# Moving the start of the settling loop and the gate steps in a streaming-encoder kernel

## The chip, the cores and the metric

The kernel is one program on one core of a Trainium2 chip. The metric is the device time of one execution in microseconds. The engines are PE (TensorE; PEld is its weight load), DVE (VectorE), ACT (ScalarE), POOL (GpSimd) and SP (SyncE). Each runs its own instructions in order and meets the others at semaphores. PE's clock has two levels, 1.2 and 2.4 GHz; the profile gives the granted clock as a share of the higher one.

## The reference

One layer of an encoder on 256 tokens of width 2048: a convolution group beside a state-space group, attention to 256 memory tokens, and a layer of single-neuron experts (PEER), with RMS norms between. The change lies in PEER. For each token and each of 8 heads, two lists of 128 keys give their 16 best; the 256 sums of the two give the 16 experts of the head. The gates are a softmax over the 16 scores, and

```python
u = jnp.take(u_tab, it, axis=0)
act = jax.nn.gelu(jnp.einsum("td,tkd->tk", xt, u))
v = jnp.take(v_tab, it, axis=0)
return jnp.einsum("tk,tkd->td", gt * act, v)
```

with tables of 16384 rows. So each token needs 128 scalar products with rows of `u_tab`, and the sum of 128 rows of `v_tab`.

## The kernel before

Tokens are handled as two halves of 128 (`tt` 0 and 1), tokens on partitions. The product with `u_tab` is split by columns.

- The first 768 columns are done densely, for all 16384 experts: `dense()` runs over 128 blocks of 128 experts. A block is loaded (`raw`, on SP's queue), transposed by PE into `ut` (6 transposes), copied from PSUM by ACT, and multiplied by the tokens (`sy`, 6 products). ACT then stores the results of two blocks at a time into two tables, `WA` for half 0 and `WB` for half 1.
- The other 1280 columns are gathered: `dot(j)` has POOL fetch one row for each token by an indirect DMA, and DVE multiplies and sums it (L895, here called a dot). There are 256 dots, 128 a half, with five gather buffers.

Before the dots of a group of heads can start, `Route` finds the chosen experts on DVE (`top16`, L789 to L797, and what follows). `gates()` ends the routing of a half: it writes `gate` from the scores, the features `fe` of the chosen indices, an exponential on ACT (L851), then on DVE a sum, a reciprocal, a product and `vidx` (L861 to L864), and on PE two transposes `ptc` (L867, L868) that ACT copies to `gT`. The features are stored to DRAM on SP (L1091) and loaded back in another layout (L906).

After the dense blocks, `settle()` picks for each token its 128 dense results out of the table. It goes by groups of 4 tokens, 32 groups a half. `extract` makes one-hot matrices E and H of the indices (matrix products `d` of 20 rows on PE, L962, then a ReLU on ACT, L964) and multiplies the table by E on PE (`y`, L970 for half 0, L973 for half 1). `pick` multiplies H by y on DVE (L980, here called a hit) and sums over partitions on PE (`more`, L982). While half 1 is settled, `left` and `build` also write half 0's coefficients back into the table (`dr`, `d`, R on DVE at L1005, `pw` on PE at L1008). Then `finish` for half 1 and its `build`s follow, and at last the dense product with `v_tab` (from L1150).

The order of the work around the change is set in two ways. DVE's order is the order in which the program calls it, written out by hand: the main loop asks for dots, and after each dot two `Pace` objects call the other generators at so many steps a dot (`ROUTE_RATE`, `DENSE_RATE`, `SETTLE_RATE`). At dot `SETTLE_AT` the settling takes the place of routing and dense work. The other engines' orders come from a planner that runs through the program with modelled times and puts each instruction where its operands are ready by the model. `LAG` is the number of groups by which `pick` runs behind `extract`. A pool's `bufs` says how many tiles of a tag may live at once: H, E, y and d have two each.

Of the kernel before, what the change touches and what calls it, by code (L numbers as in the profile page):

```python
# [9 lines left out]
F32 = mybir.dt.float32  # L10
# [4 lines left out]
AF = mybir.ActivationFunctionType  # L15
# [5 lines left out]
P = 128  # L21
# [40 lines left out]
TAIL_AT = 110  # L62
ROUTE_RATE = 4.0
DENSE_RATE = 0.8
SETTLE_RATE = 2.4
SETTLE_AT = 185
FEATS_AT = 150
LAG = 1
RAW_BUFS = 4
HI_BUFS = 3  # L70
LO_BUFS = 4
# [5 lines left out]
def trunk(ctx, tc, a, out, dbg=None):  # L77
    nc = tc.nc
    V, S, G, PE, SY = nc.vector, nc.scalar, nc.gpsimd, nc.tensor, nc.sync

    def bc(ap, shape):
        return ap.to_broadcast(shape)
# [55 lines left out]
    with ExitStack() as wctx:  # L138
        atx = wctx.enter_context(ExitStack())
        wp = wctx.enter_context(tc.tile_pool(name="wp", bufs=HI_BUFS, side="right"))  # L140
        at = atx.enter_context(tc.tile_pool(name="at", bufs=1))
# [68 lines left out]
        def run(g):  # L210
            for _ in g:
                pass
# [563 lines left out]
    class Route:  # L776
# [70 lines left out]
        def gates(self):  # L847
            self.gate = gate = rt.tile([P, PH, TOPK], F32, name="gate", bufs=2)
            gs = rt.tile([P, 2, PH], F32, name="gs")
            V.tensor_sub(gate, self.tm, bc(self.tm[:, :, 0:1], [P, PH, TOPK]))  # L850
            S.activation(gate, gate, AF.Exp)  # L851
            sq = rt.tile([P, 2, NSLOT], F32, name="sq")
            II = self.II.rearrange("p s h k -> p s (h k)")
            V.tensor_mul(sq, II, II)
            V.tensor_copy(fe[:, 0], sq)
            V.tensor_sub(fe[:, 1], sq, fe[:, 0])
            V.tensor_copy(fe[:, 2], II)
            stores.append((tick[0] + 12, self.tt))
            for _ in range(6):
                yield  # L860
            V.tensor_reduce(gs[:, 0], gate, axis=AX.X, op=ALU.add)  # L861
            V.reciprocal(gs[:, 1], gs[:, 0])
            V.tensor_mul(gate, gate, bc(gs[:, 1, :, None], [P, PH, TOPK]))
            V.tensor_scalar(vidx[self.tt], self.uidx.rearrange("p h k -> p (h k)"), float((DC - DU) // GU), None,  # L864
                            op0=ALU.add)
            pt = psu.tile([P, 2, P], F32, name="ptc", tag="pw", bufs=1)
            PE.transpose(pt[:, 0, :], gate.rearrange("p h k -> p (h k)"), ident)  # L867
            PE.transpose(pt[:, 1, :], self.II[:, 1].rearrange("p h k -> p (h k)"), ident)  # L868
            self.gT = lr_p.tile([P, 2, P], F32, name="gT", bufs=2)
            S.copy(self.gT, pt)  # L870
            yield
# [29 lines left out]
    fe_dram = [dram.tile([P, FEAT * 2 * NSLOT], BF16, name=f"fe_dram{tt}") for tt in range(NTT)]  # L901

    def load_feats(tt):
        src = fe_dram[tt].rearrange("(b j i) (f x) -> b (i f) j x", b=4, i=4, f=FEAT)
        for b in range(4):
            SY.dma_start(fe_at[tt][32 * b:32 * b + NROW].rearrange("f j s k -> f j (s k)"), src[b])  # L906
# [6 lines left out]
    fe = lr_p.tile([P, FEAT, 2, NSLOT], BF16, name="fe", bufs=1)  # L913
# [37 lines left out]
    def feats(route, g):  # L951
        p0 = 32 * (g // 8)
        return fe_at[route.tt][p0:p0 + NROW, g % 8], C[p0:p0 + NROW]

    def extract(route, g):
        psq, lr_q = settling_pools
        f, cs = feats(route, g)
        one = []
        for s, nm in ((1, "E"), (0, "H")):
            d = psq.tile([P, 4, P], F32, name="d")  # L960
            for i in range(4):
                PE.matmul(d[:, i, :], cs[:, i, :], f[:, s, :], start=i == 0, stop=i == 3, skip_group_check=True)  # L962
            one.append(lr_q.tile([P, 4, P], F32, name=nm))
            S.activation(one[-1], d, AF.Relu)  # L964
        E, H = one
        y = psq.tile([P, 4, P], F32, name="y")
        for i in range(4):
            t = 4 * g + i
            if route.tt == 0:
                PE.matmul(y[:, i, :], W[0][:, t, :], E[:, i, :], start=i == 0, stop=i == 3, skip_group_check=True)  # L970
            else:
                for h in range(2):
                    PE.matmul(y[64 * h:64 * h + 64, i, :], by_token[:, h, t, :], E[:, i, :], start=i == 0, stop=i == 3,  # L973
                              skip_group_check=True)
        return H, y

    def pick(route, g, H, y):
        if g == 0:
            route.more = psu.tile([P, NSLOT], F32, name="more", bufs=1)
        V.tensor_mul(H, H, y)  # L980
        for i in range(4):
            PE.matmul(route.more[i * NQ:(i + 1) * NQ, :], onecol[:, NQ - g:2 * NQ - g], H[:, i, :], start=g == 0,  # L982
                      stop=g == NQ - 1)

    def left(route, g):
        psq, lr_q = settling_pools
        f, cs = feats(route, g)
        dr = psq.tile([P, 4, P], F32, name="dr")
        PE.matmul(dr, f[:, 0, :], cs, start=True, stop=True)
        tag, bufs = ("L", 3) if route.tt == 0 or g % 2 else ("H", 2)  # L990
        L = lr_q.tile([P, 4, P], F32, name="L", tag=tag, bufs=bufs)
        if route.tt and g % 2:
            V.tensor_tensor(L, bc(iota[:, None, :P], [P, 4, P]), bc(route.gT[:, 1, 4 * g:4 * g + 4, None], [P, 4, P]),
                            op=ALU.is_equal)
        else:
            d = psq.tile([P, 4, P], F32, name="d")
            PE.matmul(d, f[:, 1, :], cs, start=True, stop=True)
            S.activation(L, d, AF.Relu)
        return dr, L

    def build(route, g, dr, L):
        psq, lr_q = settling_pools
        ts = slice(4 * g, 4 * g + 4)
        R = lr_q.tile([P, 4, P], F32, name="R", tag="E" if route.tt and g % 2 else "R", bufs=2)
        V.scalar_tensor_tensor(R, dr, 0.0, bc(route.cT[:, ts, None], [P, 4, P]), op0=ALU.max, op1=ALU.mult)  # L1005
        pw = psq.tile([P, 4, P], F32, name="pw", tag="y") if route.tt and g % 2 else psu.tile([P, 4, P], F32, name="pw")
        for i in range(4):
            PE.matmul(pw[:, i, :], L[:, i, :], R[:, i, :], start=i == 0, stop=i == 3, skip_group_check=True)  # L1008
        S.copy(W[route.tt][:, :, ts], pw.rearrange("p t b -> p b t"))

    routes = [Route(0), None]
# [27 lines left out]
    def settle():  # L1039
        groups = P // 4  # L1040
        for tt in range(NTT):
            held, lefts = {}, []
            for n in range(groups + LAG):
                if n < groups:
                    held[n] = extract(routes[tt], n)
                    yield
                if n >= LAG:
                    pick(routes[tt], n - LAG, *held[n - LAG])
                    yield
                if tt:  # L1050
                    if n:
                        build(routes[0], n - 1, *lefts.pop())
                    if n < groups:
                        lefts.append(left(routes[0], n))
                    yield
            if tt == 0:
                while tick[0] <= NSLOT:
                    yield
                yield from routes[0].finish()

    stores, tick = [], [0]
    routing = route_all()
    with tc.high_priority(offset=2000):
        while (0, 0) not in ready:
# [5 lines left out]
    for tt in range(NTT):  # L1070
        for g in range(len(GROUPS[tt])):
            while (tt, g) not in ready:
                next(routing)
            h0, n = routes[tt].heads(g)
            for j in range(h0 * TOPK, (h0 + n) * TOPK):
                if tick[0] == SETTLE_AT:
                    run(routing)
                    run(dense_gen)
                    psd_x.close()
                    lr_d_x.close()  # L1080
                    settling_pools += [
                        psx.enter_context(tc.tile_pool(name="psq", bufs=2, space=PSUM, reuse_waits="tile")),
                        lr_x.enter_context(tc.tile_pool(name="lr_q", bufs=2, side="right", reuse_waits="tile"))]
                    load_feats(1)
                    settling = settle()
                    paces = [Pace(settling, SETTLE_RATE)]
                routes[tt].dot(j)
                tick[0] += 1
                if stores and stores[0][0] == tick[0]:
                    tt_ = stores.pop(0)[1]  # L1090
                    SY.dma_start(fe_dram[tt_], fe.rearrange("p f s k -> p (f s k)"))  # L1091
                if tick[0] == FEATS_AT:
                    load_feats(0)
                for p in paces:
                    p()
# [115 lines left out]
```

## Time and profile before

| | |
|---|---|
| median of 3 runs | 2145.14 us (2144.22 to 2150.43) |
| profiled execution | 2155.07 us, span 2153.3 us |
| PE, PEld, DVE busy | 2030.7 (94%), 1722.3 (80%), 1709.3 (79%) us |
| ACT, POOL busy | 984.3 (46%), 763.0 (35%) us |
| mean granted clock of PE | 0.946 |

The profiled execution has 1.8 us around its span and lies 9.9 us above the median. PE is the busiest engine nearly everywhere; in the page's row of the granted clock, 40 slices of 54 us, the one slice well below full is at 1.31 to 1.47 ms, where the settling of half 0 runs. Busy shares are means over stages with different limits, so the stages are shown apart below. In the timeline a dot is a row of L895 followed by a short DVE_READ_ACCUMULATOR; matmuls in fp32 are counted as two instructions.

### The profile page before, as it was taken

To read this page: it belongs to the slowest core of one execution; us is meant where nothing else is said; L and a number is where in the kernel's file an instruction comes from. 1 tells how busy PE (TensorE), PEld (TensorE's weight loads), DVE (VectorE), ACT (ScalarE), POOL (GpSimd) and SP (SyncE) were. 2 spreads that over 40 slices of the span, in tenths; PEclk is the share of its full clock that TensorE was granted. 3 is DMA by queue.
4 is the path that set the end of the run, shared out by engine and by line. 5 is a ranking of instruction groups with operands and counts; after the bars stand their busy time and mean duration, and the time that the engine had idled before them with its cause. 6 is when DMAs were issued, how large, how long until landed. Compare 5 with 4: busy or idle time off the path is not lost.

```text
span 2153.3 us, 33240 instructions
## 1 busy us (share of the span) xinstructions
PE 2030.7 (94%) x12347; PEld 1722.3 (80%) x12347; DVE 1709.3 (79%) x2773; ACT 984.3 (46%) x1561; POOL 763.0 (35%) x576
## 2 busy tenths in 40 slices
PE   8998999997999999979999996999999999999996
PEld 7987786875899879868888885777667888888885
DVE  5889998995755568999966666556867899899998
ACT  5755666544544444323333332335654444444444
POOL 1000111000000004444555475222206777677775
PEclk9999999998999999989999996558999999999998
DMA  7656788776654658999899999456708999999996
GB/s 240 172 176 171 215 225 226 205 215 200 232 182 151 209 192 287 329 313 324 301 402 405 388 404 301 147 170 188 219 15 326 358 333 340 348 338 339 336 339 231
DMA packets 197875, 564.69 MB, mean 262 GB/s; under 512 B 31042, under 2 KB 37043, under 8 KB 197586
## 3 DMA queue, kind: packets, MB, share of 16 engines
q1 hardware_dynamic: 133842, 306.69, 42.5%
q0 software_dynamic: 63872, 255.89, 34.9%
q8 instruction: 97, 1.59, 0.3%
q14 instruction: 64, 0.52, 0.1%
HBM read 550.05 MB, written 12.45 MB: 261 GB/s over the span
## 4 chain that ended last, share of the span: by engine, by line
PE 61%; DVE 17%; issue 10%; POOL 5%; DMA 4%; ACT 2%; SPq 0%; POOLq 0%; DVEq 0%; ACTq 0%
PE acc L1159 8%; PE acc L1158 8%; PE acc L1157 8%; DVE u L895 5%; POOL u L893 5%; PE mm L195 4%; PE mm L194 4%; PE mm L196 4%; PE pw L1008 3%; PE mm L205 3%; PE mm L203 3%; PE mm L204 3%; PE y L970 3%; PE d L962 2%; PE y L973 2%
## 5 line engine op out<-in xcount | busy, mean ns | idle before, releaser
L895 DVE SCALAR_TENSOR_TENSOR u<-u,hnF 128x1280 f32<-128x1280 f32 x256 | 390.7, 1528 | 92.1 <-DMA u<-in_peer_u,uidx 89.8
L1122 POOL DMA_INDIRECT v<-in_peer_v,vidx x256 | 386.1, 1508 | 193.6 <-DVE accg L1124 84.4
L893 POOL DMA_INDIRECT u<-in_peer_u,uidx x256 | 300.8, 1175 | 397.4 <-DVE u L895 326.0
L942 PE MATMUL sy<-hnT,ut 128*128 128x256 f32 x1536 | 356.1, 384 | 22.1 <-ACT ut L938 21.0
L180 ACT CAST w_hi<-w_raw 128x1024 fp32r<-128x1024 f32 (+2 forms) x228 | 231.7, 1018 | 258.2 <-PE mm L196 124.2
L942 PEld LDWEIGHTS sy<-hnT,ut 128*128 128x128 f32 x1536 | 286.3, 192 | 62.5 <-ACT ut L938 25.0
L185 DVE TENSOR_TENSOR w_lo<-w_raw,w_hi 128x1024 fp32r<-128x1024 f32 (+2 forms) x204 | 239.7, 1177 | 106.9 <-ACT w_hi L180 106.5
L101 ACT CAST vh<-vr 128x1472 fp32r<-128x1472 f32 x128 | 183.1, 1431 | 251.9 <-PE acc L1158 207.1
L1158 PE MATMUL acc<-vh,wl 128*128 128x512 f32 (+1 forms) x768 | 295.4, 385 | 0.0
L1159 PE MATMUL acc<-vl,wh 128*128 128x512 f32 (+1 forms) x768 | 293.8, 385 | 0.5 <-DVE vl L102 0.5
L205 PE MATMUL mm<-aT_hi,w_lo 128*128 128x256 f32 x960 | 271.1, 289 | 16.2 <-DVE w_lo L185 8.3
L1157 PE MATMUL acc<-vh,wh 128*128 128x512 f32 (+1 forms) x768 | 275.7, 383 | 2.8 <-ACT vh L101 2.8
L203 PE MATMUL mm<-aT_hi,w_hi 128*128 128x256 f32 x960 | 274.2, 288 | 4.2 <-ACT w_hi L180 4.2
L204 PE MATMUL mm<-aT_lo,w_hi 128*128 128x256 f32 x960 | 271.9, 285 | 0.0
L102 DVE TENSOR_TENSOR vl<-vr,vh 128x1472 fp32r<-128x1472 f32 x128 | 216.6, 1693 | 41.6 <-ACT vh L101 39.4
L1124 DVE SCALAR_TENSOR_TENSOR accg<-v,coef,accg 128x576 f32<-128x576 f32 x256 | 208.5, 815 | 8.1 <-DMA accg<-h_dram 4.0
L205 PEld LDWEIGHTS mm<-aT_hi,w_lo 128*128 128x128 f32 x960 | 181.9, 192 | 24.3 <-DVE w_lo L185 11.3
L203 PEld LDWEIGHTS mm<-aT_hi,w_hi 128*128 128x128 f32 x960 | 184.6, 193 | 8.4 <-ACT w_hi L180 5.2
L204 PEld LDWEIGHTS mm<-aT_lo,w_hi 128*128 128x128 f32 x960 | 184.9, 193 | 2.4 <-issue 1.2
L1158 PEld LDWEIGHTS acc<-vh,wl 128*128 128x128 f32 x768 | 144.6, 188 | 30.3
L1157 PEld LDWEIGHTS acc<-vh,wh 128*128 128x128 f32 x768 | 144.6, 188 | 28.7 <-ACT vh L101 3.0
L183 POOL DMA_DIRECT2D w_lo<-in_w_kv_mem x24 | 29.3, 1221 | 384.5 <-ACT w_lo L182 277.0
(368 smaller groups left out, 3378.5 us busy)
## 6 DMA issues: line engine op xcount, KB each, us to landing
vr<-in_peer_v SPq DMA_DIRECT2D x128, 736.0 KB
raw<-in_peer_u SPq DMA_DIRECT2D x128, 384.0 KB
w_raw<-in_w_kv_mem SPq DMA_DIRECT2D x64, 512.0 KB
w_raw<-in_w_in SPq DMA_DIRECT2D x48, 512.0 KB
w_raw<-in_w_out SPq DMA_DIRECT2D x32, 512.0 KB
w_raw<-in_w_q_mem SPq DMA_DIRECT2D x32, 512.0 KB
w_raw<-in_w_o_mem SPq DMA_DIRECT2D x32, 512.0 KB
w_lo<-in_w_kv_mem POOLq DMA_DIRECT2D x24, 512.0 KB
```

Source lines behind the costliest of these rows:

```text
L180: S.copy(hi, raw)
L185: V.tensor_sub(lo, raw, hi.bitcast(F32))
L203: PE.matmul(o, wh, ah, start=first and cb % 2 == 0, stop=False, skip_group_check=True)
L204: PE.matmul(o, wh, al, start=False, stop=False, skip_group_check=True)
L205: PE.matmul(o, wl, ah, start=False, stop=last and end, skip_group_check=True)
L893: G.indirect_dma_start(out=u, out_offset=None, in_=a["peer_u"].rearrange("e (q c) -> (e q) c", c=GU), in_offset=bass.IndirectOffsetOnAxis( ...
L895: V.scalar_tensor_tensor(u, u, 1.0, hnF[:, self.tt, :], op0=ALU.mult, op1=ALU.mult, accum_out=self.act[:, j:j + 1])
L942: PE.matmul(ps[:, b % 2, :], ut[:, k, :], hnT[:, k, :], start=k == 0 and b % 2 == 0, stop=k == KD - 1 and b % 2 == 1, skip_group_check=True)
L1122: G.indirect_dma_start(out=v, out_offset=None, in_=table, in_offset=bass.IndirectOffsetOnAxis(ap=vidx[tt][:, j:j + 1], axis=0))
L1157: PE.matmul(o, wh[:, tt, :], vh[:, cs_], start=b == 0, stop=False)
L1158: PE.matmul(o, wl[:, tt, :], vh[:, cs_], start=False, stop=False)
L1159: PE.matmul(o, wh[:, tt, :], vl[:, cs_], start=False, stop=b == NB - 1)
```

## The change

The settling starts at dot 176 in place of 185, at 2.2 steps a dot in place of 2.4. For half 0 picks run two groups behind the extracts in place of one; for half 1 still one. For groups 2 and 3 of every four of half 0, H takes the buffers of tag R and y those of tag dr, which the settling of half 0 does not use otherwise, so that four H and four y can live at once. Of the gate steps, the exponential and the store of the features are asked for 16 dots after the scores are ready (the store was asked for 12 dots later, the exponential at once), the DVE steps 4 dots after that, and the transposes 16 dots later again.

```diff
-SETTLE_RATE = 2.4
-SETTLE_AT = 185
+SETTLE_RATE = 2.2
+SETTLE_AT = 176
-LAG = 1
+LAG = (2, 1)
+DELAY = 16
...
-            S.activation(gate, gate, AF.Exp)
...
-            stores.append((tick[0] + 12, self.tt))
-            for _ in range(6):
+            tasks.append((tick[0] + DELAY, self.softmax(gs)))
+            yield
+
+        def softmax(self, gs):
+            gate = self.gate
+            S.activation(gate, gate, AF.Exp)
+            SY.dma_start(fe_dram[self.tt], fe.rearrange("p f s k -> p (f s k)"))
+            for _ in range(4):
                 yield
             V.tensor_reduce(gs[:, 0], gate, axis=AX.X, op=ALU.add)
...
+            for _ in range(DELAY):
+                yield
             pt = psu.tile([P, 2, P], F32, name="ptc", tag="pw", bufs=1)
...
+        spread = route.tt == 0 and g % 4 > 1
...
-            one.append(lr_q.tile([P, 4, P], F32, name=nm))
+            one.append(lr_q.tile([P, 4, P], F32, name=nm, tag="R" if spread and nm == "H" else nm))
...
-        y = psq.tile([P, 4, P], F32, name="y")
+        y = psq.tile([P, 4, P], F32, name="y", tag="dr" if spread else "y")
...
-                if n >= LAG:
-                    pick(routes[tt], n - LAG, *held[n - LAG])
+                if n >= lag:
+                    pick(routes[tt], n - lag, *held[n - lag])
...
+                    for _, task in tasks:
+                        run(task)
...
-                if stores and stores[0][0] == tick[0]:
...
+                for at, task in tasks:
+                    if tick[0] >= at:
+                        next(task, None)
```

On DVE, after half 1's gate steps, the first hits (H) stood behind 113 further dots, the 187th dot of the program being the last before them:

```order
L863 TENSOR_TENSOR gate<-gate,gs 128x128
L864 TENSOR_SCALAR vidx_8372<-uidx 128x128
L895 SCALAR_TENSOR_TENSOR u,act<-u,hnF 128x1280 x113
L980 TENSOR_TENSOR H<-H,y 128x512
L895 SCALAR_TENSOR_TENSOR u,act<-u,hnF 128x1280
L980 TENSOR_TENSOR H<-H,y 128x512 x2
```

Now the same rows read so; half 1's gate steps come 17 dots later, and the first hit follows the 178th dot:

```order
L869 TENSOR_TENSOR gate<-gate,gs 128x128
L870 TENSOR_SCALAR vidx_8372<-uidx 128x128
L903 SCALAR_TENSOR_TENSOR u,act<-u,hnF 128x1280 x87
L989 TENSOR_TENSOR H<-H,y 128x512
L903 SCALAR_TENSOR_TENSOR u,act<-u,hnF 128x1280
L989 TENSOR_TENSOR H<-H,y 128x512
```

The first hit moved nine dots forward. Counted on, the 32nd hit follows dot 206 (before 212), the 33rd dot 209 (before 216), the 64th and last dot 251 (before 254).

On ACT, where the dense work of half 0's gate steps stands, the exponential came behind the copy of the 23rd block's `ut`, and the copy of `gT` behind that of the 26th:

```order
L938 COPY ut<-ut 128x768 x2
L851 ACT_TABLE_LOAD
L851 ACTIVATE gate<-gate 128x128
L945 COPY WA<-sy 128x128x2
L946 COPY WB<-sy 128x128x2
L938 COPY ut<-ut 128x768 x2
L945 COPY WA<-sy 128x128x2
L946 COPY WB<-sy 128x128x2
L938 COPY ut<-ut 128x768
L870 COPY gT<-ptc 128x256
```

Now these rows are:

```order
L946 COPY ut<-ut 128x768 x2
L863 ACT_TABLE_LOAD
L863 ACTIVATE gate<-gate 128x128
L953 COPY WA<-sy 128x128x2
L954 COPY WB<-sy 128x128x2
L946 COPY ut<-ut 128x768 x2
L953 COPY WA<-sy 128x128x2
L954 COPY WB<-sy 128x128x2
L946 COPY ut<-ut 128x768 x2
```

The exponential of half 0 has not moved: the planner still puts it behind the 23rd `ut`. The copy of `gT` has gone from behind the 26th to behind the 43rd. Half 1's exponential has come forward by one block, from behind the 59th `ut` to behind the 58th, and its `gT` has gone back from the 62nd to the 73rd.

On PE, the transposes of half 0's gates stood behind the 26th block's transposes:

```order
L942 MATMUL sy<-hnT,ut 128x256 x6
L936 MATMUL ut<-ident,raw 128x128 x6
L867 MATMUL ptc<-ident,gate 128x128
L868 MATMUL ptc<-ident,II 128x128
L942 MATMUL sy<-hnT,ut 128x256 x6
```

Now they stand behind the 43rd block's, in a stretch that reads alike:

```order
L950 MATMUL sy<-hnT,ut 128x256 x6
L944 MATMUL ut<-ident,raw 128x128 x6
L875 MATMUL ptc<-ident,gate 128x128
L876 MATMUL ptc<-ident,II 128x128
L950 MATMUL sy<-hnT,ut 128x256 x6
```

That is 17 blocks later, while the DVE steps that they wait for went from behind dot 35 to behind dot 53. Half 1's went from behind the 62nd block's transposes to behind the 72nd block's products, and their DVE steps from behind dot 74 to behind dot 91. In the settling, PE's order had the products y of two groups ahead of the first `more`; now it has those of four. On SP the store of half 0's features still stands behind the 27th `raw`, that of half 1 behind the 63rd (before the 64th).

## Rows read from the trace of the kernel before

**Rows 1.** Windows by stage: busy us of PE, PEld, DVE, ACT, POOL, clock, DMA, GB/s.
```profile
850.00:1303.00 453.00, 428.09 (x2310) 376.01 (x2310) 366.15 (x763) 144.94 (x261) 240.80 (x188) 0.98 0.96 355
1303.00:1325.00 22.00, 5.50 (x51) 3.90 (x50) 14.74 (x21) 3.92 (x8) 12.72 (x11) 0.68 0.98 313
1325.00:1432.00 107.00, 105.89 (x712) 80.61 (x712) 56.74 (x83) 32.19 (x58) 26.29 (x27) 0.50 0.57 177
...
1468.00:1570.00 102.00, 98.24 (x1133) 70.17 (x1129) 80.98 (x121) 61.88 (x110) 27.18 (x29) 1.00 0.64 194
```

**Rows 2.** Timeline as the dense work ends: start, us, engine, line, operation [idle before <-releaser].
```profile
1303.14 0.61 PE L962 MATMUL d<-hnF,C 20*128 20x128 bf16 x8
...
1303.64 1.49 DVE L895 SCALAR_TENSOR_TENSOR u<-u,hnF 128x1280 f32<-128x1280 f32 x1 [0.54 <-DMA u<-in_peer_u,uidx]
...
1304.45 1.16 PE L970 MATMUL y<-E,WA 128*128 128x128 f32 x8
...
1306.62 1.16 PE L970 MATMUL y<-E,WA 128*128 128x128 f32 x8 [0.46 <-ACT E L964]
...
1313.24 1.49 DVE L895 SCALAR_TENSOR_TENSOR u<-u,hnF 128x1280 f32<-128x1280 f32 x1 [2.79 <-DMA u<-in_peer_u,uidx]
...
1325.28 0.68 DVE L980 TENSOR_TENSOR H<-H,y 128x512 f32<-128x512 f32 x1
...
1326.11 0.65 PE L982 MATMUL more<-H,onecol 128*32 128x128 f32 x8 [15.76 <-DVE H L980]
```

**Rows 3.** Windows of 5 us: the clock's fall in settling and at its end.
```profile
1310.00:1315.00 5.00, 0.35 (x4) 0.17 (x3) 1.96 (x4) 0.00 (x0) 0.94 (x1) 0.60 1.05 293
...
1565.00:1570.00 5.00, 4.29 (x41) 2.42 (x40) 3.54 (x5) 3.04 (x6) 0.00 (x0) 1.00 0.00 0
1570.00:1575.00 5.00, 3.31 (x11) 2.35 (x12) 4.56 (x9) 0.54 (x2) 0.00 (x0) 0.54 0.50 153
```

**Rows 4.** Timeline of DVE: three hits of half 0, the last being its 32nd.
```profile
1396.66 0.69 DVE L980 TENSOR_TENSOR H<-H,y 128x512 f32<-128x512 f32 x1 [1.46 <-PE y L970]
...
1400.21 0.69 DVE L980 TENSOR_TENSOR H<-H,y 128x512 f32<-128x512 f32 x1 [1.46 <-issue]
...
1432.19 0.69 DVE L980 TENSOR_TENSOR H<-H,y 128x512 f32<-128x512 f32 x1 [2.87 <-PE y L970]
```

**Rows 5.** Timeline of DVE: the 33rd hit, the 64th, and the last two dots.
```profile
1443.26 0.68 DVE L980 TENSOR_TENSOR H<-H,y 128x512 f32<-128x512 f32 x1
...
1566.46 0.69 DVE L980 TENSOR_TENSOR H<-H,y 128x512 f32<-128x512 f32 x1 [2.62 <-PE y L973]
...
1567.67 1.48 DVE L895 SCALAR_TENSOR_TENSOR u<-u,hnF 128x1280 f32<-128x1280 f32 x1
...
1569.07 1.49 DVE L895 SCALAR_TENSOR_TENSOR u<-u,hnF 128x1280 f32<-128x1280 f32 x1
```

**Rows 6.** Timeline: the two exponentials on ACT, and PE behind each.
```profile
938.66 0.31 ACT L851 ACTIVATE gate<-gate 128x128 f32<-128x128 f32 x1 [14.60 <-DVE gate L850]
...
940.26 5.49 PE L942 MATMUL sy<-hnT,ut 128*128 128x256 f32 x12 [11.89 <-ACT ut L938]
...
1063.50 0.31 ACT L851 ACTIVATE gate<-gate 128x128 f32<-128x128 f32 x1 [8.76 <-DVE gate L850]
...
1065.10 4.54 PE L942 MATMUL sy<-hnT,ut 128*128 128x256 f32 x12 [4.76 <-ACT ut L938]
```

**Rows 7.** Timeline: dots 53 and 91, block 43's and 73's transposes, one gate step.
```profile
942.76 0.28 DVE L861 TENSOR_REDUCE gs<-gate 128x8 f32<-128x128 f32 x1
...
998.07 2.56 DVE L895 SCALAR_TENSOR_TENSOR u<-u,hnF 128x1280 f32<-128x1280 f32 x1
...
1001.07 0.82 PE L936 MATMUL ut<-ident,raw 128*128 128x128 f32 x6
...
1105.48 1.49 DVE L895 SCALAR_TENSOR_TENSOR u<-u,hnF 128x1280 f32<-128x1280 f32 x1
...
1105.97 0.82 PE L936 MATMUL ut<-ident,raw 128*128 128x128 f32 x6
```

More of the change, by code (lines that the diff above doesn't have):

```diff
@@ L1042, in settle @@
             held, lefts = {}, []
-            for n in range(groups + LAG):
+            lag = LAG[tt]
+            for n in range(groups + lag):
                 if n < groups:
@@ L1059, in settle @@
                 yield from routes[0].finish()
-    stores, tick = [], [0]
+    tasks, tick = [], [0]
     routing = route_all()
@@ L1088, in trunk @@
                 tick[0] += 1
-                if stores and stores[0][0] == tick[0]:
-                    tt_ = stores.pop(0)[1]
-                    SY.dma_start(fe_dram[tt_], fe.rearrange("p f s k -> p (f s k)"))
+                for at, task in tasks:
+                    if tick[0] >= at:
+                        next(task, None)
                 if tick[0] == FEATS_AT:
```

## The prediction

> **What bounds the kernel now.** I read the windows by stage first, then the timeline across their borders, then the waits. From 850 to 1303 us the dense work runs, and PE is busy 428.09 of 453 us at a clock of 0.98 [rows 1]. Then come 22 us in which PE does 5.50 us of work, and 107 us in which it is busy throughout, but at the lower of its two levels: 0.50, that is 1.2 GHz. The second half of the settling runs at 1.00, again with PE the busiest: 98.24 of 102 us, DVE 80.98. So each stage hangs on PE, and the weak spot is the join. The timeline shows why [rows 2]. PE starts the settling at 1303.14, has two groups' y done by 1308 and then finds its next instruction, a `more`, waiting 15.76 us for DVE: the hit stands behind dot 187 in DVE's order, and DVE gets there at 1325.28, one dot after another. The clock falls while PE waits (0.60 over 1310 to 1315, so about 1 us at full and 4 at half) [rows 3], and does not come back in half 0. At half clock a group takes 3.55 us, 1396.66 to 1400.21 [rows 4].
>
> **The gate steps.** The orders shown above decide this part more than the diff does. What stands in the way now is the exponential on ACT: it waits 14.60 us for DVE with the copies of `ut` behind it, and PE loses 11.89 us; half 1's waits 8.76 us and PE loses 4.76 [rows 6]. Half 0's exponential does not move, so its 11.89 us stay. Half 1's moves one block forward. PE then runs out of `ut` one block earlier, 453/128 = 3.5 us, less what DVE gains by having one dot fewer ahead of the scores (0 to 1.4 us, since the reductions in front wait for POOL's products anyway) and less the two table copies that no longer stand between the exponential and the next `ut`. I take +1.4 us; the ends are 0 and +3.5. The transposes on PE are new in their places. Half 0's wait for DVE's steps behind dot 53: 998.07 + 2.56 and three steps of up to 0.28 give 1001.5, with some six routing steps more and four gate steps fewer ahead of it than now, say 1002.7; PE comes there after block 43's transposes, at 1001.7 [rows 7]. That is a new wait of 1 us (0 to 3), with all the dense work queued behind it. Half 1's: dot 91 begins at 1105.48, its steps end near 1107.8, and PE is there one block after 1105.97, at 1109: nothing. The store on SP stays where it is for half 0 and comes one `raw` earlier for half 1, where four buffers of `raw` hide it; without them it would cost PE the same few us as the exponential. Sum: the dense work ends 2.5 us later, PE's first d of the settling is at 1305.6; ends -1 and +8.
>
> **The first hits.** Dot 178 begins at 1303.64 [rows 2] and takes 1.40 us until the next instruction can start, as the last two dots do (1567.67, 1569.07) [rows 5]. So DVE stands before the first hit at 1305.1. The first y ends 2.4 us after the first d (1305.5 now), so the first hit is at 1308.0 in place of 1325.28. DVE waits 3 us there; the dots queued behind it are covered, since PE sets the pace. What is late next is the pace of PE. The 15.76 us wait goes: PE's order has four y ahead of the first `more`, which last until about 1314.5, and by then DVE has two or three hits done. One more thing stands in this place: dots 179 to 182 wait for their gathers, up to 2.79 us before the one at 1313.24, while the features of half 1 are loaded. That holds DVE to four hits in 12 us; four y of lead on PE just cover it.
>
> **The pace of half 0 at full clock** is not in the trace beyond two groups. From below, DVE: 28 dots of 1.40 and 32 hits of 0.6 (1566.46 to 1567.67 holds a hit and R) are 58.4 us, 1.83 a group. From above, for a clock that holds, the two y of the same loop, 1304.45 and 1306.62: 2.17. I take 2.1, near the second, since it is this loop with this chain (d, ReLU, y). Then the 32nd hit is at 1308.0 + 31 x 2.1 = 1373, now 1432.19 [rows 4]: 59 us earlier.
>
> **The rest.** From the 32nd to the 33rd hit there are three dots in place of four: -1.4 us on 11.1. From the 33rd to the 64th I keep 1443.26 to 1566.46 [rows 5], 123.2 us: 42 dots stand there in place of 38, 5.6 us that lie in DVE's idle time (21 us in 102); if that cover were gone they would be paid. After the last hit five dots are left in place of two: +4.2 us, bare, since half 1's `finish` needs them all. From dot 256 on nothing is changed. In all -59 - 1.4 + 4.2 = -56 us: a span of 2097, 2099 us with the 1.8 us around it. The median stands 9.9 us below the profiled execution, so 2089 us.
>
> **Rivals.**
>
> *The clock falls in the first groups all the same.* For it: while PE has only d and y to do it issues a y every 2.17 us and stands in between for ACT's ReLU. In the present run the clock fell about 1 us after the last d, so what PE had done in the us before counted for little; at 1570 it fell to 0.54 after 5 us in which PE had been busy 4.29 [rows 3]; and once down it stayed down for 107 us with PE busy 105.89. Against it: in half 1, with the same kinds of instructions, it holds at 1.00 for 102 us. Price: four y at full clock, done at 1314.5, then 28 groups of 3.55 us: the 32nd hit is at 1414, 18 us earlier, and -18 - 1.4 + 4.2 = -15 us, so 2130 us (2124 to 2139 with the dense work's ends).
>
> *It falls later in half 0*, at a gather that comes late. In the middle, 16 groups cost 1.45 us more each: 2112 us.
>
> *The transposes stand as long as the exponential does* (the slower side). The planner's DVE is ahead of the real one by 14.60 and 8.76 us at the exponentials [rows 6]; if it is so at both moved transposes, PE stands 11.89 us twice and runs the products behind at half clock (12 in 5.49 us, some 2.7 us too many), 29 us in place of the 2.5 counted. With the clock down in half 0 as above that is -15 + 27 = +12 us: 2157 us. It decides from a dense work that ends over 17 us later. Against it: PE has just been set back 11.89 us when it gets there, and the dots counted in rows 7 leave 1 us.
>
> *The change does not do what it says*: for the exponential that is settled by the order above, and in the sum. For the first hits it would be so if the dense work ended before about 1296, when PE's four y would be used up before dot 178; nothing here makes it earlier.
>
> The Trainium skill ("TensorE: Matmul & The Clock Gate", Part 1) says that idleness takes TensorE's clock down and sustained activity brings it back. By that rule the first forecast holds, as PE no longer stands; the trace agrees where PE stood idle, at 1310, and disagrees for the 107 us that PE spent busy at 0.50. So I give the first rival nearly as much as the forecast.
>
> **How the numbers follow.** Clock held: 0.50, 2089 us, own range 2076 to 2099 (1.83 to 2.17 a group, the dense work's ends). Clock falls at once: 0.34, 2130. Falls later: 0.10, 2112. Transposes: 0.06, 2157. What a measurement of this kernel can tell from no change is 0.3%, 6.4 us. Only the upper end of the second case lies within it, so faster 0.87, same 0.07, slower 0.06. The range reaches from the forecast's lower end into the second case up to its upper part, 2077 to 2138.
>
> **What the profile would show.** Right: PE at a granted clock of 1.00 from the dense work's end on, no `more` waiting over 3 us, hits of half 0 some 2.1 us apart, the 32nd near 1373, dot 256 near 1514. The exponential of half 0 still waiting some 14 us. Wrong in size: hits 3.55 us apart from about 1315 and the 32nd near 1414. Wrong in kind: PE waiting at `ptc` for several us in the dense stretch, or the dense work ending past 1315.

## The result, and the profile after

The changed kernel takes 2117.37 us (median of 4 runs, 2111.73 to 2124.71), the kernel before beside it 2147.78: a ratio of 0.986, with a 95% interval of 0.9818 to 0.9902. Twelve later executions of it have a median of 2124.14. The forecast was 2089 with 2077 to 2138 as its range: the direction and the range held. Of the 56 us forecast 30 came in these runs, and 24.5 by the later medians (2148.65 for the kernel before). The profiled execution took 2112.99 us, its span 2111.2, its mean granted clock 0.962 (before 0.946).

Windows of the changed kernel, which answer to [rows 1] (columns as there):

```profile
850.00:1299.00 449.00, 427.16 (x2317) 375.69 (x2317) 361.68 (x764) 145.52 (x263) 240.19 (x188) 0.98 0.97 358
1298.70:1311.70 13.00, 9.53 (x97) 7.69 (x96) 10.68 (x15) 6.69 (x13) 5.29 (x6) 1.00 1.02 334
1312.00:1376.00 64.00, 64.00 (x439) 48.62 (x437) 34.97 (x52) 19.77 (x35) 15.92 (x17) 0.50 0.59 183
1377.00:1403.00 26.00, 23.89 (x283) 17.42 (x282) 19.21 (x29) 14.50 (x27) 8.43 (x9) 1.00 0.79 248
1414.00:1520.00 106.00, 104.03 (x1215) 75.19 (x1211) 91.37 (x137) 64.54 (x115) 36.38 (x39) 1.00 0.81 254
1524.00:1540.00 16.00, 10.86 (x40) 8.17 (x41) 8.82 (x16) 3.30 (x7) 0.00 (x0) 0.50 0.15 47
```

The 22 us in which PE did 5.50 us of work are gone: it is busy 9.53 of the 13 us that follow the dense work. The clock falls all the same, but the stretch at 0.50 is 64.9 us long by the trace's record of the clock (1311.7 to 1376.6), where before it was 157 (1311.0 to 1468.0, so some three slices of the page's row and not one). A new wait stands in the last row. The timeline at the join, which answers to [rows 2], on PE and DVE:

```profile
1298.66 0.62 PE L971 MATMUL d<-hnF,C 20*128 20x128 bf16 x8
...
1299.97 1.16 PE L979 MATMUL y<-E,WA 128*128 128x128 f32 x8 [0.69 <-ACT E L973]
...
1301.69 0.68 DVE L989 TENSOR_TENSOR H<-H,y 128x512 f32<-128x512 f32 x1
...
1306.60 1.16 PE L979 MATMUL y<-E,WA 128*128 128x128 f32 x8 [0.52 <-ACT E L973]
...
1309.95 0.38 PE L971 MATMUL d<-hnF,C 20*128 20x128 bf16 x4 [0.74 <-ACT E L973]
1310.26 0.43 PE L991 MATMUL more<-H,onecol 128*32 128x128 f32 x8
1310.61 1.16 PE L979 MATMUL y<-E,WA 128*128 128x128 f32 x8
1311.70 0.60 PE L971 MATMUL d<-hnF,C 20*128 20x128 bf16 x4
```

The first hit stands at 1301.69 (before 1325.28), and the first `more` waits for nothing (before 15.76 us). Until 1310 PE has only d and y, and stands for ACT's ReLU before each y and before the last two d's. DVE's hits, which answer to [rows 4, 5], and the last dot:

```profile
1368.90 0.69 DVE L989 TENSOR_TENSOR H<-H,y 128x512 f32<-128x512 f32 x1 [2.87 <-PE y L979]
1372.45 0.69 DVE L989 TENSOR_TENSOR H<-H,y 128x512 f32<-128x512 f32 x1 [1.46 <-PE y L979]
...
1378.80 0.69 DVE L989 TENSOR_TENSOR H<-H,y 128x512 f32<-128x512 f32 x1 [0.27 <-PE y L979]
1381.03 0.69 DVE L989 TENSOR_TENSOR H<-H,y 128x512 f32<-128x512 f32 x1
...
1396.64 0.69 DVE L989 TENSOR_TENSOR H<-H,y 128x512 f32<-128x512 f32 x1
1405.82 0.68 DVE L989 TENSOR_TENSOR H<-H,y 128x512 f32<-128x512 f32 x1
...
1518.50 0.69 DVE L989 TENSOR_TENSOR H<-H,y 128x512 f32<-128x512 f32 x1 [1.44 <-PE y L982]
...
1526.56 1.49 DVE L903 SCALAR_TENSOR_TENSOR u<-u,hnF 128x1280 f32<-128x1280 f32 x1
```

Two paces can be read here: 3.55 us a group while the clock is at 0.50, 2.23 once it is at 1.00. The sum of the prediction, against this execution:

| stretch | before | forecast | after |
|---|---|---|---|
| first d of the settling | 1303.14 | 1305.6 | 1298.66 |
| first hit | 1325.28 | 1308.0 | 1301.69 |
| 1st to 32nd hit | 106.9 | 65 | 94.95 |
| 32nd to 33rd | 11.1 | 9.7 | 9.2 |
| 33rd to 64th | 123.2 | 123.2 | 112.7 |
| 64th hit to dot 256 | 2.6 | 6.8 | 8.1 |
| dot 256 to the end | 584.2 | 584.2 | 584.6 |

So 42.1 us of the span went where 56 were forecast. The row that misses most, by 30 us, is the one in which the clock is at 0.50; the first hit (6.3 us earlier than forecast) and the 33rd to 64th hit (10.5 us shorter) made up for half of it.

How that clock comes out differs between executions of one kernel, and the time with it. Of 52 executions of the kernel before, timed beside the experiments, 48 took 2143 to 2163 us at mean clocks of 0.940 to 0.952, and 4 took 2113.6 to 2122.7 at 0.964 to 0.970. The changed kernel's sixteen: 14 took 2111.7 to 2126.2 at 0.957 to 0.962, two took 2137.4 and 2142.6 at 0.950 and 0.945. An interval counts only runs within 1.5% of the fastest of their kernel, which leaves out 14 of the 21 runs of before beside `e5_changed_again`, where three of those 4 stand, and 2 of the 11 beside `e1_start_only`, where the fourth does; so the medians of all runs are compared below, and intervals are given where none of the four stands beside. Beside the medians a fit stands over 134 executions (one level for each kernel, one common slope against the time at 0.50, which is twice the share that the mean clock lacks times the span): 1 us less at 0.50 goes with 0.35 us less time.

### The profile page after: what moved, and what is told of

Its sections match the earlier page's. It is cut to its first block, busy times and chain, and to the rows that moved or that the text cites. A ratio compares the mean times of both kernels' runs of the same rounds, so it can differ in the third digit from the quotient of the medians.

```text
span 2111.2 us, 33235 instructions
## 1 busy us (share of the span) xinstructions
PE 2005.8 (95%) x12347; PEld 1705.1 (81%) x12347; DVE 1705.1 (81%) x2773; ACT 985.0 (47%) x1561; POOL 762.4 (36%) x576
## 4 chain that ended last, share of the span: by engine, by line
PE 70%; DVE 14%; DMA 6%; issue 5%; ACT 4%; POOL 1%; SPq 0%; DVEq 0%; ACTq 0%; POOLq 0%
PE sy L950 8%; PE acc L1170 8%; PE acc L1171 8%; PE acc L1169 8%; DVE u L903 5%; PE mm L196 4%; PE mm L195 4%; PE mm L197 4%; PE pw L1017 3%; PE mm L206 3%; PE mm L204 3%; PE mm L205 3%; PE y L979 2%; DMA w_lo<-in_w_kv_mem 2%; PE d L971 2%
## 5 line engine op out<-in xcount | busy, mean ns | idle before, releaser
L901 POOL DMA_INDIRECT u<-in_peer_u,uidx x256 | 296.1, 1156 | 366.3 <-DVE u L903 280.7
```

The lines of the kernel that those rows point to most:

```text
L901: G.indirect_dma_start(out=u, out_offset=None, in_=a["peer_u"].rearrange("e (q c) -> (e q) c", c=GU), in_offset=bass.IndirectOffsetOnAxis( ...
```

## The experiments

The theory: the change closes the gap at the join and shortens the stretch at 0.50; the clock falls because of what PE does in the first groups, and that is where the forecast failed. Rivals: the earlier start is all of it; the gate steps carry a good part; the clock's fall has to do with PE's waits and not with what it computes.

**One part at a time.** `e1_start_only` sets the two constants in the kernel before; `e2_lag_only` takes over the lead; `e3_start_lag` both; `e4_gates_only` only the gate steps.

```diff
 # e1_start_only, against the kernel before (e3 too)
-SETTLE_RATE = 2.4
-SETTLE_AT = 185
+SETTLE_RATE = 2.2
+SETTLE_AT = 176
 # e2_lag_only, against the kernel before (e3 too)
-LAG = 1
+LAG = (2, 1)
...
+        spread = route.tt == 0 and g % 4 > 1
...
 # e4_gates_only, against the kernel before
+            tasks.append((tick[0] + DELAY, self.softmax(gs)))
...
 # e7_one_group, against the changed kernel
-LAG = (2, 1)
+LAG = (1, 1)
-        spread = route.tt == 0 and g % 4 > 1
+        spread = route.tt == 0 and False
```

> Kernel before with the start of the settling alone moved (dot 176, 2.2 steps a dot); picks one group behind, gate steps as before. Theory (the gain is the 22 us gap at the join, and on top of it a clock that comes back early only with the two-group lead): dot 178 starts at 1303.6, the first hit at 1308; the clock falls near 1311 as it does in the changed kernel and stays at 0.50 to the end of half 0, as in the kernel before; 31 hits of 3.55 us put the 32nd at about 1417, 15 us earlier than before, and the time is about 2132 us. Rival A (the earlier start is all of it): the clock comes back in half 0 as in the changed kernel, the 32nd hit is near 1400, and the time about 2120. Rival B (one group of lead doesn't cover the dots that wait for their gathers, so that PE waits at the join all the same): within 5 us of before.

> Kernel before with the two-group lead of half 0 alone (picks two groups behind, H and y of groups 2 and 3 of every four in the buffers of R and dr); start at dot 185 and gate steps as before. Theory: PE has four y done and then waits for the hit behind dot 187, so the first hit is at 1325 as before and the clock has fallen by 1311; it comes back after some 22 hits, as in the changed kernel: 21 x 3.55 + 10 x 2.2 = 97 us, the 32nd hit at about 1422, 10 us earlier, and the time about 2138 us. Rival A (the earlier start is all of it): no change, 2148. Rival B (the clock's return hangs on the phase of the dots and gathers, not on the lead): it stays at 0.50 for half 0 and the time is within 3 us of before.

> The changed kernel with the gate steps as before (exponential at once, store 12 dots later, transposes not put off): start and lead without the delay. Theory: the dense work ends 4.5 us later than in the changed kernel, at 1303.1 as before, all else as there: about 2122 us. Rival (the gates' delay carries a good part of the gain, by way of a dense work that ends earlier or a DVE that is free at the join): 2130 or more.

> Kernel before with the gate steps alone put off by 16 dots; start at dot 185, one group of lead. Theory: half 1's exponential costs PE 2.2 us in place of 4.76, the first d of the settling is at 1298.7 in place of 1303.1, dot 178 at 1300.2 in place of 1303.6; the first hit still stands behind dot 187 on DVE, so 3 to 4.5 us are kept: about 2144 us. Rival (the delay carries a good part of the gain): 2135 or less. Rival of my own blind sum: dense work 2.5 us later, 2150.

The changed kernel itself, `e5_changed_again`, was timed beside `e7_one_group`, which has start and gate steps without the lead, on another chip than the four above.

> The changed kernel unaltered, timed beside the others on one chip, since executions of one kernel differ by up to 35 us with their mean clock (the kernel before: 2122.67 at 0.967, 2149.94 at 0.949). Theory (start 9 us, gate steps some 3 us, and a lead that shortens the stretch at 0.50 in many executions): median 2118, mean clocks 0.957 to 0.963. Rival (the four runs of the changed kernel were a lucky draw, and it is start and lead without the delay again): 2130 to 2135, clocks near 0.952.

> The changed kernel with picks one group behind in half 0 too (no lead, H and y with two buffers): start and gate steps alone. Theory (the lead's part is a shorter stretch at 0.50): the first hit at 1302 to 1305 as in the changed kernel, PE without a wait over 3 us at the join, but 0.50 for all of half 0 in most executions, mean clocks 0.945 to 0.95; 2136 us. Rival (the lead gives nothing): as the changed kernel beside it, 2118.

| kernel | median us (runs) | median clock | at equal clock, against before |
|---|---|---|---|
| before | 2148.65 (52) | 0.948 | 0 |
| start (`e1`) | 2141.99 (6) | 0.947 | -9 ± 3 |
| lead (`e2`) | 2143.03 (6) | 0.951 | 0 ± 3 |
| gates (`e4`) | 2141.17 (6) | 0.950 | -3 ± 3 |
| start, gates (`e7`) | 2135.14 (9) | 0.950 | -11 ± 2 |
| start, lead (`e3`) | 2133.11 (6) | 0.953 | -7 ± 3 |
| all three (`e5`) | 2124.14 (12) | 0.960 | -8 ± 2 |

The last column is the level of the fit, with twice its standard error. By the medians each part alone gives 7.5 us or less, where its six executions range over 20 to 44 us; none carries the gain. The start is a saving at equal clock, as it should be where a wait goes. The lead gives nothing at equal clock, but with it the clock is higher: 0.960 against 0.950 beside `e7_one_group`, and 11 us less time.

Against what was expected: `e4_gates_only` (2144) and `e7_one_group` (2136) came out within 3 us, and the 2150 of the prediction's sum for the gate steps missed. `e1_start_only` came out 10 us over its 2132, though its 32nd hit stood where the theory put it, and `e5_changed_again` 6 us over its 2118, at the clocks expected. `e2_lag_only` came out 5 us over its 2138, and in its profile the clock stays at 0.50 for all of half 0 (1313.6 to 1443.3), as rival B had it and not the theory. `e3_start_lag` missed its 2122 and met the number of its rival, 2130 or more; but at equal clock it lies within 1 us of the changed kernel, so what sets the two apart is the clock.

Windows of `e3_start_lag`, then of `e7_one_group`, over their stretches at 0.50:

```profile
1314.00:1433.00 119.00, 118.03 (x808) 88.33 (x809) 65.43 (x97) 39.33 (x72) 31.27 (x31) 0.50 0.53 170
```

```profile
1303.00:1449.00 146.00, 145.00 (x973) 108.05 (x967) 80.32 (x117) 47.64 (x87) 37.20 (x37) 0.50 0.56 179
```

In these executions the gap is closed and the clock stays at 0.50 for all of half 0, with PE busy 99%: the prediction's first rival. Its 32nd hit at 1414 is met by `e1_start_only` (1416.2) and `e3_start_lag` (1413.6). The changed kernel's own profile differs by the clock's return at 1376.6. PE there:

```profile
1372.28 1.03 PE L971 MATMUL d<-hnF,C 20*128 20x128 bf16 x8
1373.23 1.08 PE L991 MATMUL more<-H,onecol 128*32 128x128 f32 x16
1374.25 2.08 PE L979 MATMUL y<-E,WA 128*128 128x128 f32 x8
1376.26 0.76 PE L971 MATMUL d<-hnF,C 20*128 20x128 bf16 x8
```

It is the one place of half 0 at which the products `more` of two groups stand together. `e5_changed_again` came back there too (1387.4, its 16 `more` at 1384.04), but `e3_start_lag` has two such places in its order and `e2_lag_only` one (1356.6), and neither kernel came back there. So what brings the clock back in the middle of half 0 isn't settled.

**What the clock hangs on.** d is a product over 20 rows of the 128. `e6_full_rows` sets the other rows to zero and runs half 0's d's over all of them: the same sums, the same number of matmuls.

```diff
+    Cz = [x[:, :2 * 4 * P].rearrange("p (b i k) -> p b i k", b=2, i=4) for x in (
+        fe.rearrange("p f s k -> p (f s k)"), room[1][:, NQ * NSLOT // 4:].bitcast(BF16))]
...
+            G.memset(fe_at[0], 0.0)
...
+        if route.tt == 0:
+            f, cs = fe_at[0][:, g % 8], Cz[g // 16][:, g // 8 % 2]
 # e12_first_groups, in its place
+        if route.tt == 0 and g < 8:
+            f, cs = fe_at[0][:, g], Cz[0][:, 0]
```

> The changed kernel, with one thing more: in half 0 the products d run over all 128 rows in place of 20 (C padded with zeros for each of the four row blocks, the unused rows of the features set to zero), so that the same number of matmuls of the same 128 columns gives the same sums. Theory (the clock falls in the first groups because d keeps PE busy with 20 rows of 128 and y alone isn't enough; the forecast of 2089 failed there and nowhere else): granted clock 1.00 through half 0, hits 2.2 us apart, the 32nd some 68 us after the first in place of 95, time 2086 to 2092, and little spread between executions. Rival A (rows don't matter, the clock falls because PE stands for ACT's ReLU between the first y): 0.50 again from about 1311 and 2112 to 2125 us. Rival B (full rows make the weight loads or d slower): d longer than 0.61 us for 8, and a gain below 10 us.

It took 2094.17 us (7 runs, 2091.05 to 2103.55), 30 less than the changed kernel beside it and 2 over the theory's upper end. In its profile the clock is at 1.00 from before the join to 1382.1, past the 32nd hit, which follows the first by 66.3 us: 2.14 a group. `e12_first_groups` gives only the first eight groups their 128 rows:

> e6_full_rows with d over 128 rows in the first 8 groups of half 0 alone; the other 24 groups have 20 rows as in the changed kernel. It asks whether only the first groups lose the clock. Theory (the blind forecast's: a loop of 20-row d's that comes in at full clock keeps it, as it does in half 1 and from 1376.6 to 1403.9 in the changed kernel): granted clock 1.00 to the end of half 0, hits 2.15 to 2.2 us apart, 2094 to 2098 us. Rival (the loop of half 0 loses the clock wherever rows are 20): 1.00 up to the eighth group, near 1325, then 0.50 and 3.55 us a group, with a return after the two `more` in a row near the 22nd hit in many executions; 2108 to 2118 us.

It took 2093.67 us (5 runs, 2087.69 to 2096.25; ratio to before 0.9733, 0.9707 to 0.9759), with hits 2.25 us apart over half 0. Windows of it, over its first 13 us of settling, over the 24 groups of 20 rows, and behind half 0:

```profile
1305.00:1318.00 13.00, 9.15 (x98) 7.83 (x97) 8.36 (x12) 6.68 (x13) 3.74 (x4) 1.00 0.56 177
1324.00:1384.00 60.00, 55.77 (x662) 41.51 (x659) 48.77 (x73) 31.56 (x58) 21.54 (x23) 1.00 0.82 266
1384.00:1395.00 11.00, 9.39 (x68) 6.13 (x70) 11.00 (x17) 4.16 (x9) 7.23 (x5) 0.53 0.58 185
```

And rows of PE's timeline, the d of the first group, two of PE's waits behind it, and the first d with 20 rows:

```profile
1305.02 0.61 PE L986 MATMUL d<-hnF,fe 128*128 128x128 bf16 x8
...
1308.49 1.16 PE L994 MATMUL y<-E,WA 128*128 128x128 f32 x8 [0.46 <-ACT E L988]
...
1316.28 0.38 PE L986 MATMUL d<-hnF,fe 128*128 128x128 bf16 x4 [0.74 <-ACT E L988]
...
1323.51 0.61 PE L986 MATMUL d<-hnF,C 20*128 20x128 bf16 x8
```

Both kinds take 0.61 us for 8. In the first 13 us PE has the same order of d, y and `more` as in the changed kernel, waits as long for the ReLU (0.46 to 0.80 us here, 0.46 to 0.74 there) and is busy 9.15 us, in the changed kernel 9.53; there the clock then falls, here it holds. From 1324 on the 20-row loop runs for 60 us at 1.00. The same loop that comes in at 0.50 stays there with PE busy 64.00 of 64 us. So the first eight groups decide, and in them what PE computes rather than how it waits; the rival by which waits for the ReLU take the clock down falls. One thing more differs in the first 13 us, the DMA engines (0.56 of their time busy, 1.02 in the changed kernel). `e11_rows_both` below, with full rows too, has them nearly as busy, and the clock holds:

```profile
1299.00:1312.00 13.00, 9.15 (x98) 7.81 (x97) 9.87 (x16) 6.69 (x13) 4.69 (x5) 1.00 0.90 315
```

**The change beside a clock that holds.** With d over 128 rows in half 0, `e8_rows_alone` is otherwise the kernel before, `e9_rows_one_group` has start and gates, `e10_rows_no_gates` start and lead. `e11_rows_both` is a try at more: rows for half 1 too, its features loaded at the seventh group, 2.1 steps a dot.

```diff
 # e11_rows_both, against e6_full_rows
-SETTLE_RATE = 2.2
+SETTLE_RATE = 2.1
...
-                    load_feats(1)
...
+            load_feats(1)
+        f, cs = fe_at[route.tt][:, g % 8], Cz[g // 16][:, g // 8 % 2]
```

> The kernel before, with d of half 0 over 128 rows (as in e6_full_rows) as the only edit: start at dot 185, one group of lead, gates as before. It gives what the change is worth when the clock can hold. Theory (rows carry the clock; the gap at the join is a separate cost): the first hit at 1325 behind dot 187 as before, a fall of the clock in PE's wait and a return within some 10 us, then 2.14 us a group: the 32nd hit near 1393 (before 1432), 33 to 64 some 9 us shorter, 2098 to 2104 us, so that the whole change is worth 5 to 10 us beside e6_full_rows. Rival A (the clock, once down at the join, stays down for half 0 even with full rows): 2135 or more. Rival B (the gap costs its full 17 us even at full clock): 2110.

> e6_full_rows with picks one group behind in half 0 (start and gate steps kept). Theory (the lead acts through the clock alone): no difference from e6_full_rows, 2094, hits 2.14 us apart. Rival (the lead also covers hits that come late on DVE, behind dots that wait for gathers): pace 2.3 or more in half 0, 2099 or more.

> e6_full_rows with the gate steps as in the kernel before (start and lead kept). Theory (the delay saves 2 to 3 us in the dense stretch): 2096 to 2097. Rival (it saves nothing, and the earlier end of the dense work in the profiled run of the changed kernel was chance): 2094. Rival of the blind sum (it costs 2.5 us): 2091.

> A try at a faster version: e6_full_rows, with d of half 1 over 128 rows too, half 1's features loaded at the seventh group and no longer at the join, and 2.1 settling steps a dot in place of 2.2. Theory: of the 13.7 us at 0.50 around the turn of the halves and the 10 us at the end some 5 to 10 go (0.35 us of time each), and two dots fewer stand bare behind the last hit (2.8 us): 2088 to 2091. Rival (the clock there falls because PE waits, whatever the rows; DVE is the bound between): 2092 to 2096.

| kernel, rows in half 0 | median us (range) | ratio to before, interval |
|---|---|---|
| before (`e8`) | 2104.42 (2102.18 to 2104.61) | 0.9787 (0.9760 to 0.9814) |
| start, gates (`e9`) | 2096.96 (2095.77 to 2101.93) | 0.9757 (0.9729 to 0.9784) |
| start, lead (`e10`) | 2098.91 (2096.38 to 2099.66) | 0.9759 (0.9733 to 0.9786) |
| all three (`e6`) | 2094.17 (2091.05 to 2103.55) | three of the 4 runs stand beside it |
| all three, `e11_rows_both` | 2093.85 (2085.79 to 2104.53) | 0.9748 (0.9719 to 0.9777) |

So the rows alone give the kernel before 44 us, more than the whole change, and beside them the change is worth 10, a difference between two chips on which the kernel before took 2148.08 and 2146.95. In `e8_rows_alone` the gap still takes the clock down, and it comes back at once (windows, and PE's wait in the timeline):

```profile
1310.00:1320.00 10.00, 7.38 (x61) 5.69 (x59) 5.99 (x9) 3.92 (x8) 5.62 (x6) 1.00 0.94 298
1320.00:1330.00 10.00, 6.09 (x55) 4.75 (x56) 8.55 (x13) 2.28 (x4) 3.73 (x4) 0.66 1.02 356
1330.00:1390.00 60.00, 52.31 (x646) 41.79 (x644) 50.96 (x76) 29.45 (x54) 21.27 (x23) 1.00 0.79 256
```

```profile
1323.91 0.66 PE L999 MATMUL more<-H,onecol 128*32 128x128 f32 x8 [4.67 <-DVE H L997]
```

The stretch at 0.50 is 6.8 us here, and 157 with 20 rows. PE's wait was shorter too, 4.67 us for 15.76, since the dense work ended 9 us later in this execution; but with 20 rows the clock stays down also where no such wait stands (130 us in `e1_start_only`). Of the rest, the gate steps look like 3 to 5 us saved (2098.91 against 2094.17, on different chips). The lead is worth 3 or nothing (2096.96 against 2094.17, ranges that overlap), so that its 11 us of above came by the clock; the rival has a grain of truth, as hits of `e9_rows_one_group` are 2.30 apart over half 0 in place of 2.14, and DVE waits for y at 18 of them in place of 4. `e11_rows_both` is no faster than `e6_full_rows`, as its rival had it: its profile has the fall at the turn of the halves as before (17.1 us at 0.50 from 1378.6), though no longer the one at the end. By their medians all six kernels with full rows are faster than the kernel before and the changed one.

## Why the prediction was right, and where it was wrong

*The wait at the join*: right. The first `more` waits 0 in place of 15.76 us, four y cover the late gathers, and the first hit comes 3.0 us behind the first d (2.4 forecast). `e1_start_only` shows that one group of lead covers them as well.

*The clock in half 0*: the step of the forecast that failed. The case that was given 0.50 was a clock that holds; it fell at 1311.7, 13 us behind the first d, where before it fell at 1311.0, 8 us behind it. The first rival named the place, the groups in which PE has only d and y. Of its reasons the waits for the ReLU fall, as shown above; what counted were the 20 rows of d. The argument against it was that half 1 holds 1.00 with the same kinds of instructions. That was true and didn't bear on it: half 1's loop holds the products of `left` and `build` too, and it even brings a lost clock back (at 1468.0 before, at 1414.1 now), which half 0's did only in part. That these products are what holds it was not tested. `e12_first_groups` bears this out: with the first groups' d over 128 rows the forecast's case comes about, 2093.67 us for 2089. The first rival was right on the fall and wrong on its length: 28 groups at 3.55 us were counted, and in the profile of the changed kernel it was some 18, with 9 at 2.23 behind them. The two executions at 2137 and 2143 us, at the clocks of the kernels that stay down, are probably that rival in full; they have no trace.

That the time lies in the range is in part luck. The range held because it took in the first rival's 2130, and the time fell between the two cases by a return of the clock in the middle of half 0 that no case had and that isn't settled. The third case's 2112 is near for no reason of its own, since the clock didn't fall late but at once.

The Trainium skill's rule ("TensorE: Matmul & The Clock Gate", Part 1), that sustained activity brings the clock back, stands in the prediction. In `e8_rows_alone` the trace agrees with it, 6.8 us after a fall; in the changed kernel it disagrees for 64 us, as before for 107.

*The pace at full clock*: right within 0.15 us a group. 2.1 was taken between 1.83 and 2.17; 2.14 is measured in `e6_full_rows`, and 2.23 in the changed kernel and 2.25 in `e12_first_groups`, a little above the upper end. (The forecast's own range follows from its terms as 2077 to 2097, not 2076 to 2099.)

*The gate steps*: wrong in sign, a term of +2.5 us that measures -2 to -4 in the profiles. The ends of -1 and +8 don't follow from its parts either, which give 0 to +6.5. The exponential of half 0 stays, as the order said (columns: start, duration, engine, and the wait in brackets, which answer to [rows 6, 7]):

```profile
939.00 0.31 ACT L863 ACTIVATE gate<-gate 128x128 f32<-128x128 f32 x1 [14.42 <-DVE gate L851]
940.59 1.65 PE L950 MATMUL sy<-hnT,ut 128*128 128x256 f32 x3 [11.71 <-ACT ut L946]
...
1000.86 0.29 DVE L869 TENSOR_TENSOR gate<-gate,gs 128x128 f32<-128x128 f32 x1
...
1001.39 0.82 PE L944 MATMUL ut<-ident,raw 128*128 128x128 f32 x6
...
1002.05 0.27 PE L875 MATMUL ptc<-ident,gate 128*128 128x128 f32 x1
...
1058.80 0.31 ACT L863 ACTIVATE gate<-gate 128x128 f32<-128x128 f32 x1 [6.75 <-DVE gate L851]
1059.84 2.42 PE L950 MATMUL sy<-hnT,ut 128*128 128x256 f32 x10 [2.21 <-ACT ut L946]
```

Half 0's product of the gates ends at 1001.15 and PE takes the transposes 0.9 us later without a wait, where 1 was counted (in `e5_changed_again` it waits 0.40). Half 1's exponential was to cost PE 1.4 us more and costs 2.21 in place of 4.76: DVE is there 4.7 us earlier, more than the one dot that the sum gave it. What this comes to can be read from the transposes of the first and the 75th block, of the kernel before and then of the changed one:

```profile
850.68 2.82 PE L936 MATMUL ut<-ident,raw 128*128 128x128 f32 x12 [0.93 <-ACT WB L753]
...
1115.06 1.47 PE L936 MATMUL ut<-ident,raw 128*128 128x128 f32 x12
```

```profile
851.02 2.82 PE L944 MATMUL ut<-ident,raw 128*128 128x128 f32 x12 [0.93 <-ACT WB L754]
...
1111.36 1.47 PE L944 MATMUL ut<-ident,raw 128*128 128x128 f32 x12
```

That is 264.4 us before and 260.3 now. All profiles agree: up to this block the gate steps save some 4 us (260.4 in `e4_gates_only`, 264.4 in `e1_start_only`), 2.4 in `e5_changed_again`, and 3 with full rows. From there to the first d the profiles differ by 10 us (186.5 to 196.1), with PE's waits for `raw`, and the first block itself comes anywhere from 846.2 to 854.4, so that the first d of the settling lies anywhere from 1293.8 to 1312.1 in the profiles of the twelve experiments. The early first d of the changed kernel's profile, and with it the early first hit, is thus in part chance. The third rival, transposes that stand as long as the exponential, has nothing in its favour.

*From the 33rd to the 64th hit*: 123.2 us were kept and 112.7 measured. [Rows 1] had the reason in view: the clock of before came back at 1468, 25 us behind the 33rd hit, and those 25 us were part of the 123.2. Now it comes back at 1414, 8 us behind that hit.

*Behind the last hit*: +5.5 us for +4.2. PE now waits for the dots before the transposes of `finish`:

```profile
1528.20 0.77 PE L885 MATMUL ptc<-ident,act 128*128 128x128 f32 x2 [5.58 <-DVE u L903]
```

The clock falls in that wait and stays at 0.50 to 1540.4, 17.1 us in place of 6.8; from dot 256 to the end it still took 584.6 us, so no more than the dots was lost.

## What to carry to other kernels

Where a stage runs at the lower clock with its engine busy throughout, price the engine's entry into the stage before its loop: the groups that decide may be the first few, and an edit that only moves waits can leave the clock where it was. A product over few of the rows can be filled with zeros to all of them at no time of its own, here for 30 to 44 us. And a change whose gain hangs on the clock is to be timed over many executions, with the mean clock of each beside its time.

## What the runs showed of the hardware

With the d's of eight groups over 128 rows in place of 20 (`e12_first_groups`), at the same 0.61 us for 8, the granted clock of the whole half 0 was 1.00 in place of 0.50. The same 20-row loop ran for 60 us at 1.00 where it came in at 1.00 (`e12_first_groups`), and for 64 us at 0.50 where it came in at 0.50 (the changed kernel), each time with PE busy over nine tenths of it. What ended the 64 us is open.
